# RG-LRU in a hybrid decoder block: the second gelu projection between the gates of the two blocks, with weights split up to two pieces ahead

## The chip, the cores and the metric

The kernel runs on one core of a Trainium2 chip. Its engines are TensorE (PE, with its weight loads listed as PEld), VectorE (DVE), ScalarE (ACT), GpSimd (POOL) and SyncE (SP), which here only issues loads. Each engine works through a queue of its own in a fixed order, and semaphores tie the queues together. Matrix products land in PSUM, which DVE and ACT can read. The metric is the time of one execution on the device, in microseconds, as the median of several runs.

## The reference

One decoder block on a sequence of 512 tokens, with 16 meta tokens ahead of them and a width of 1024. Two token mixers, HGRN2 and RG-LRU, read the same normalised input; their outputs are merged by sigmoid gates, and a mixture of 32 experts follows. The part that the change touches is the RG-LRU:

```python
    xc = conv(xb) + conv_b                       # causal, depthwise, width 4
    r = sigmoid(einsum('btni,nij->btnj', xh, w_r) + b_r)   # 8 blocks of 128
    i = sigmoid(einsum('btni,nij->btnj', xh, w_i) + b_i)
    log_a = -8 * r * softplus(-lam)
    a = exp(log_a)
    u = sqrt(-expm1(2 * log_a)) * (i * xc)
    h = scan(h_t = a_t * h_{t-1} + u_t)
    return h * gelu(yb)
```

Here `xb` and `yb` are 1024 columns each of the projection of the normalised input, called lx and ly below.

## The kernel before

Tokens lie along the free dimension and channels along the partitions. A projection of 128 channels takes eight steps of 128 input channels. For precision each operand of a large product is split into a high and a low part, and three products are added: high times high, high times low, low times high. The normalised input stays in buffers, split, for the whole mixer (`hnH`, `hnL`).

Weights come in pieces of 128 columns. The class `Weights` holds them in the order of use: `load` issues a load of two pieces (1 MB) on SP's queue into one of two `raw` buffers, and `prep` splits the next piece into one of three `hl` tiles, which are used in turn. In the RG-LRU the high half is a cast on ScalarE (L88) and the low half a subtraction on POOL (L91); in the merge behind it the cast is on DVE (L90). `dense` (L196) takes a ready piece, multiplies, and calls `prep` once when it is halfway through, so that the next piece is being split while the present one is in use. Gate weights of two blocks, for r and i, form one piece of half the width.

`lru` (L622) goes over the 8 blocks in pairs. For a pair it emits the projections lx of both blocks, whose output is convolved on DVE (L650) and split (L88, L91); then the tail of the pair before, called `finish` (L690): logarithms and exponentials on ScalarE, a product (L703), the scan over time (L704), a product with the gelu (L705) and a split on DVE, whose low half is on POOL; then the projections ly of both blocks, whose output becomes the gelu in four instructions, alternately on ScalarE and DVE (L673 to L676); then the gates of both blocks. `gates` (L656) fills four PSUM tiles with 12 short matmuls (L663); ScalarE reads them with a tanh (L665) into `RR` (r) and `iv` (i), and DVE multiplies (L667). `RR` and `TH` are one buffer each, which the tail of a pair reads and the gates of the next pair write.

All PSUM tiles come from one pool of eight. One lx output takes two, one ly output one, the gates of one block four. Between these steps the loop at L714 lets the last two heads of the HGRN2 take a step, one every five steps of the projections: a step multiplies scores for one level into a tile that is kept for two levels (L545, read on DVE in L561), in the first four levels a product of states into a tile of its own (L550, read in L553 or L555), and at the end the head's output (L566, L567, read in L576).

The framework plans the order on each engine when the kernel is built: the program's order is its priority, but an instruction that it believes to be held up lets later ones pass, and it gives PSUM tiles out in the order that it plans. So the convolution of lx (L650), which the program has ahead of the tail, stands between the tail's L703 and L704 in the trace.

After the RG-LRU comes the merge (L799): gate projections, projections of both mixers' outputs, and the output projection. As its buffers come free, the loads of the experts' weights start. Then come the routing and the experts.

Of the kernel before, what the change touches and what calls it, by code (L numbers as in the profile page):

```python
# [19 lines left out]
M = 16  # L20
N = T + M
D = 1024
KD = D // 128
# [7 lines left out]
PARTS = ((0, 256), (256, 528))  # L31
# [7 lines left out]
def hybrid_block_kernel(ctx: ExitStack, tc: tile.TileContext, x, meta, norm1_g, w_in, hg_lb,  # L39
# [21 lines left out]
    def add_slots(pool, names):  # L61
        for n in names:
            pool_of[n] = pool
            free.append(n)

    def uniq(name):
        seq[0] += 1
        return f"{name}_{seq[0]}"

    def slot(shape, dtype, name):  # L70
        s = free.pop(0)
        return pool_of[s].tile(shape, dtype, name=uniq(name), tag=s), s
# [4 lines left out]
    def ms(tag, shape, dtype, name):  # L77
        return misc.tile(shape, dtype, name=uniq(name), tag="m" + tag)

    def ps(shape, name, dtype=F32):  # L80
        return psum.tile(shape, dtype, name=name, tag="ps")
# [4 lines left out]
    def split(hi, lo, src, he, le):  # L86
        if he is ACT:
            ACT.activation(hi, src, AF.Copy)  # L88
        else:
            he.tensor_copy(hi, src)  # L90
        le.tensor_sub(lo, src, hi.bitcast(F32))  # L91
# [87 lines left out]
    W = Weights()  # L179
# [13 lines left out]
        W.columns(wub, 128 * j, DVE, POOL)  # L193
    W.rows(wout2, 128 * (KD - 2), DVE, POOL)

    def dense(outs, cols_, nk, aH, aL):  # L196

        wh, wl = W.next()
        for k in range(nk):
            if k == nk // 2:  # L200
                W.prep()
            for w, a in ((wh, aH), (wh, aL), (wl, aH)):
                for o, (c0, c1) in zip(outs, cols_):
                    PE.matmul(o[:, :c1 - c0], w[:, k, :], hsl(a, k, c0, c1),  # L204
                              start=(k == 0 and w is wh and a is aH),
                              stop=(k == nk - 1 and w is wl))
            yield

    def proj(all_tokens, use, parts=PARTS):
        if all_tokens:  # L210
            pp = [ps([128, b - a], "pj") for a, b in parts]
            yield from dense(pp, parts, KD, hnH, hnL)
            use(pp)
        else:
            p_ = ps([128, 512], "pj")
            yield from dense([p_], [(M, N)], KD, hnH, hnL)
            use(p_)

    def interleave(main, sides, every):
# [22 lines left out]
    hnH, hnL, hn_s = [], [], []  # L242
    for i in range(2):
        a, s = slot([128, 4, N], F32R, "hnH")
        b, s2 = slot([128, 4, N], F32R, "hnL")
# [4 lines left out]
    def hsl(lst, k, a, b):  # L250
        return lst[k // 4][:, k % 4, a:b]
# [85 lines left out]
    def col(nm, i=None):  # L337
        a, b = R[nm]
        return cols[:, a:b] if i is None else cols[:, a + i:a + i + 1]
# [264 lines left out]
    def add_ob():  # L604
        for lst, nm in ((obH, "obH"), (obL, "obL")):
            t_, s = slot([128, 4, T], F32R, nm)
            lst.append(t_)
            ob_s.append(s)
# [4 lines left out]
    def end_heads():  # L613

        for g_ in sides:
            run(g_)
        sides.clear()
        tp.__exit__(None, None, None)
        late = ctx.enter_context(tc.tile_pool(name="late", bufs=1, side="right", reuse_waits="tile"))
        add_slots(late, [f"t{i}" for i in range(NLATE)])  # L620

    def lru():  # L622
        L2 = ms("F", [128, 2, N], F32, "l2")
        iv = L2[:, 0]
        tail = None

        gp = tc.tile_pool(name="gelu", bufs=1, reuse_waits="tile")
        pool_of["g"] = gp.__enter__()
        for b0 in range(0, NB, 2):
            bs = (b0, b0 + 1)  # L630
            XC = ms("AH"[b0 // 2 % 2], [128, 2, N], F32, "xc")
            RR = ms("C", [128, 2, N], F32, "r")
            TH = ms("D", [128, 2, N], F32, "th")
            GE = (ms("E", [128, 2, T], F32, "ge") if b0 % 4 else
                  pool_of["g"].tile([128, 2, T], F32, name=uniq("ge"), tag="g"))
            XH = {}
            WG = []

            def use_lx(b):
                def f(pp):  # L640

                    xc = XC[:, b - b0]
                    for (a, c), p_ in zip(PARTS, pp):
                        ACT.activation(xc[:, a:c], p_[:, p_.shape[1] - (c - a):], AF.Identity,
                                       scale=col("cw", 24 + b), bias=col("cb", b))
                    for d in range(1, 4):
                        for (a, c), p_ in zip(PARTS, pp):
                            n = p_.shape[1]
                            o = xc[:, max(a, d):c]
                            DVE.scalar_tensor_tensor(o, p_[:, n - d - o.shape[1]:n - d], col("cw", 8 * (3 - d) + b), o,  # L650
                                                     op0=OP.mult, op1=OP.add)
                    xh = XH[b] = ms("BG"[b - b0], [128, 2, N], F32R, "xh")
                    split(xh[:, 0], xh[:, 1], xc, ACT, DVE)
                return f

            def gates(b):  # L656
                xh, i = XH[b], b - b0
                r, th = RR[:, i], TH[:, i]
                for gi, dst in enumerate((r, iv)):
                    pg = [ps([128, 272], "pg") for _ in PARTS]  # L660
                    for w, a in ((0, 0), (0, 1), (1, 0)):
                        for (c0, c1), p_ in zip(PARTS, pg):
                            PE.matmul(p_[:, :c1 - c0], WG[w][:, 2 * gi + i], xh[:, a, c0:c1], start=(w == 0 and a == 0), stop=(w == 1))  # L663
                    for (c0, c1), p_ in zip(PARTS, pg):
                        ACT.activation(dst[:, c0:c1], p_[:, :c1 - c0], AF.Tanh, scale=0.5, bias=hb[:, 8 * gi + b:8 * gi + b + 1])  # L665
                ACT.activation(th, r, AF.Tanh, scale=C4[:, b:b + 1], bias=C4[:, b:b + 1])
                DVE.scalar_tensor_tensor(XC[:, i], iv, 1.0, XC[:, i], op0=OP.add, op1=OP.mult)  # L667

            def use_ly(b):
                def f(p_):  # L670

                    c, ge = math.sqrt(2 / math.pi), GE[:, b - b0]
                    ACT.activation(ge, p_, AF.Square, scale=math.sqrt(0.044715 * c))  # L673
                    DVE.scalar_tensor_tensor(ge, ge, c, p_, op0=OP.add, op1=OP.mult)
                    ACT.activation(ge, ge, AF.Tanh)
                    DVE.scalar_tensor_tensor(ge, ge, 1.0, p_, op0=OP.add, op1=OP.mult)  # L676
                return f

            for b in bs:
                yield from proj(True, use_lx(b), PARTS4)  # L680
            if tail:
                tail()
            for b in bs:
                yield from proj(False, use_ly(b))
            WG += W.next()
            W.prep()
            for b in bs:
                gates(b)
                yield
            def finish(b0=b0, bs=bs, XC=XC, RR=RR, TH=TH, GE=GE):  # L690
                for i in range(2):
                    ACT.activation(L2[:, i], TH[:, i], AF.Ln, bias=1.0)
                    ACT.activation(TH[:, i], TH[:, i], AF.Ln, scale=2.0, bias=tiny)
                    DVE.tensor_sub(TH[:, i], TH[:, i], L2[:, i])
                if b0 == 4:
                    end_heads()
                    add_ob()
                for i, b in enumerate(bs):

                    av, u, ge = RR[:, i], TH[:, i], GE[:, i]  # L700
                    ACT.activation(av, av, AF.Exp, scale=NC4[:, b:b + 1], bias=NC4[:, b:b + 1])
                    ACT.activation(u, u, AF.Exp, scale=0.5, bias=nln2)
                    DVE.tensor_mul(u, u, XC[:, i])  # L703
                    DVE.tensor_tensor_scan(u, av, u, 0.0, op0=OP.mult, op1=OP.add)  # L704
                    DVE.scalar_tensor_tensor(ge, ge, 0.5, u[:, M:], op0=OP.mult, op1=OP.mult)  # L705
                    split(obH[b // 4][:, b % 4], obL[b // 4][:, b % 4], ge, DVE, POOL)

            tail = finish
        tail()
        gp.__exit__(None, None, None)  # L710
        late2 = ctx.enter_context(tc.tile_pool(name="late2", bufs=1, reuse_waits="tile"))
        add_slots(late2, ["u0"])
# [16 lines left out]
    def tk(lst, t, a=0, b=D):  # L729
        return lst[t // 2][:, t % 2, a:b]  # L730
# [389 lines left out]
    for p in range(last_p + 1):  # L1120
# [15 lines left out]
        if p == last_p:  # L1136
            gfb = ms("A", [128, D], F32, "gfb")
            for half in range(2):
                p_ = ps([128, 4, 128], "pgf")
# [27 lines left out]
    outs = [slot([128, D], F32, "o") for t in range(4)]  # L1167
# [12 lines left out]
    for t in range(4):  # L1180
        p_, hs = ps([128, 512], "pcb"), tk(h32, t, 512)
# [89 lines left out]
```

## Time and profile before

| | |
|---|---|
| median of 3 runs | 1009.46 us (1008.91 to 1009.81) |
| profiled execution, its own time | 1012.21 us |
| its span, from the first to the last instruction | 1010.4 us |
| mean granted TensorE clock | 0.968 |
| PE busy | 941.5 us (93%) |
| DVE busy | 449.7 us (45%) |
| ACT busy | 256.0 us (25%) |
| POOL busy | 246.1 us (24%) |
| read from memory | 250.89 MB |

Busy shares are averages over stages that differ: the mixer up to about 300 us, the merge to 486 us, and the experts. All times in rows below are microseconds from the start of the span. A granted clock of 1.00 is 2.4 GHz and 0.50 is 1.2 GHz; a value between is a mix of the two in a stretch.

### The profile page before, as it was taken

How to read it: one execution, taken by the hardware profiler on the slowest of the kernel's cores; microseconds unless marked ns; L12 is line 12 of the kernel's file. 1: busy time of each engine (PE TensorE's matmuls, PEld its weight loads, DVE VectorE, ACT ScalarE, POOL GpSimd, SP SyncE). 2: the span in 40 equal slices, each digit the busy share in tenths (PEclk: the TensorE clock that was granted, in tenths of full speed). 3: DMA queues.
4: the chain of work that ended last, by engine and by line, in shares of the span. 5: the costliest groups of instructions: out<-in, count | busy, mean ns of one | idle time of the engine just before them, and what ended most of it. 6: DMA issues, size and time to landing. Idle time of an engine off the chain costs nothing.

```text
span 1010.4 us, 12299 instructions
## 1 busy us (share of the span) xinstructions
PE 941.5 (93%) x4812; PEld 608.2 (60%) x4812; DVE 449.7 (45%) x931; ACT 256.0 (25%) x456; POOL 246.1 (24%) x167
## 2 busy tenths in 40 slices
PE   7989999979898999999949999999999999989885
PEld 6979998868876888888833444434334343433331
DVE  5667548767583333333442333333343343323323
ACT  6445536855860000000401010101101010110014
POOL 4543441334446454545300000000000000000002
PEclk9999999979898999999959999999999999999998
DMA  6221112212176231316978999999999999999992
GB/s 213 85 84 43 43 53 84 71 35 84 53 262 222 63 125 63 125 63 247 384 296 293 409 408 408 408 408 408 409 409 409 408 408 408 409 408 408 408 355 88
DMA packets 94297, 251.76 MB, mean 249 GB/s; under 512 B 6581, under 2 KB 39433, under 8 KB 94234
## 3 DMA queue, kind: packets, MB, share of 16 engines
q1 hardware_dynamic: 91352, 244.61, 63.5%
q0 software_dynamic: 2304, 4.20, 1.1%
q10 hardware_dynamic: 578, 2.10, 0.5%
q8 instruction: 40, 0.66, 0.3%
q14 instruction: 23, 0.19, 0.1%
HBM read 250.89 MB, written 4.19 MB: 252 GB/s over the span
## 4 chain that ended last, share of the span: by engine, by line
PE 76%; DVE 8%; DMA 7%; ACT 4%; POOL 2%; issue 2%; SPq 0%; POOLq 0%; DVEq 0%; ACTq 0%
PE pj L204 26%; PE put L1009 11%; PE pgt L1009 9%; PE py L1028 9%; PE pcb L1042 6%; DMA wx<-in_w_up_dram 6%; PE po L794 3%; PE pl L545 2%; PE pw L971 2%; PE pxs L1001 1%; PE po L1066 1%; PE pj L311 1%; POOL hl L91 1%; DVE th L703 1%; PE pht L1022 1%
## 5 line engine op out<-in xcount | busy, mean ns | idle before, releaser
L204 PE MATMUL pj<-hnH,hl 128*128 128x512 f32 (+1 forms) x960 | 253.7, 355 | 5.1 <-POOL hl L91 5.1
L91 POOL TENSOR_TENSOR hl<-raw,hl 128x1024 fp32r<-128x1024 f32 (+1 forms) x76 | 175.9, 2318 | 208.1 <-ACT hl L88 107.0
L204 PEld LDWEIGHTS pj<-hnH,hl 128*128 128x128 f32 x960 | 165.8, 195 | 29.3 <-POOL hl L91 6.9
L204 PE MATMUL pj<-hnL,hl 128*128 128x512 f32 (+1 forms) x480 | 150.0, 351 | 0.0
L1045 DVE TENSOR_TENSOR h<-h,pcb 128x512 f32<-128x512 f32 x124 | 77.5, 681 | 112.6 <-PE pcb L1042 112.6
L1009 PE MATMUL put<-wx,XS 128*64 128x512 f32 x512 | 121.1, 600 | 3.4 <-DMA wx<-in_w_up_dram 3.4
L1009 PE MATMUL pgt<-wx,XS 128*64 128x512 f32 x512 | 119.6, 606 | 1.9 <-DMA wx<-in_w_gate_dram 1.9
L978 POOL DMA_INDIRECT XG<-HD,idx x16 | 16.5, 1029 | 411.7 <-DVE sw L987 252.6
L1028 PE MATMUL py<-wx,HG 128*64 128x512 f32 x512 | 113.8, 596 | 0.7 <-ACT HG L1023 0.7
L204 PEld LDWEIGHTS pj<-hnL,hl 128*128 128x128 f32 x480 | 86.1, 194 | 10.2
L1009 PEld LDWEIGHTS pgt<-wx,XS 128*64 128x64 f32 x512 | 36.0, 139 | 71.1 <-issue 63.2
L1028 PEld LDWEIGHTS py<-wx,HG 128*64 128x64 f32 x512 | 35.2, 137 | 66.2 <-issue 61.1
L1009 PEld LDWEIGHTS put<-wx,XS 128*64 128x64 f32 x512 | 33.6, 136 | 67.3 <-issue 62.8
L1042 PE MATMUL pcb<-Y,OHT 128*128 128x512 f32 x248 | 68.1, 411 | 0.0
L1042 PEld LDWEIGHTS pcb<-Y,OHT 128*128 128x128 f32 x248 | 43.5, 188 | 39.3 <-issue 30.8
L1036 DVE SCALAR_TENSOR_TENSOR Y<-py,sw,Y 128x512 fp32r<-128x512 f32 x31 | 23.3, 751 | 91.7 <-ACT Y L1035 90.6
L90 DVE CAST hl<-raw 128x1024 fp32r<-128x1024 f32 (+1 forms) x40 | 31.7, 793 | 66.4 <-PE pj L204 64.6
L1023 ACT ACTIVATE HG<-pht 128x512 f32<-128x512 f32 x16 | 9.6, 598 | 182.5 <-PE pht L1022 182.4
L1035 ACT ACTIVATE Y<-py,sw 128x512 fp32r<-128x512 f32 x31 | 21.3, 688 | 102.5 <-PE py L1028 98.6
L204 PE MATMUL pj<-obH,hl 128*128 128x512 f32 x128 | 40.7, 394 | 0.0
L1014 ACT ACTIVATE HG<-pgt,sw 128x512 f32<-128x512 f32 x16 | 11.0, 687 | 107.4 <-PE pgt L1009 107.4
L88 ACT ACTIVATE hl<-raw 128x1024 fp32r<-128x1024 f32 (+1 forms) x36 | 36.1, 1006 | 7.1 <-PE pj L311 3.2
(259 smaller groups left out, 1116.5 us busy)
## 6 DMA issues: line engine op xcount, KB each, us to landing
wx<-in_w_up_dram SPq DMA_DIRECT2D x64, 1024.0 KB, 18.4
wx<-in_w_gate_dram SPq DMA_DIRECT2D x62, 1024.0 KB, 18.3
wx<-in_w_down_dram SPq DMA_DIRECT2D x60, 1024.0 KB, 19.0
raw<-in_w_in_dram SPq DMA_DIRECT2D x24, 1024.0 KB, 5.2
raw<-in_w_up_b_dram SPq DMA_DIRECT2D x4, 1024.0 KB
raw<-in_w_out_dram SPq DMA_DIRECT2D x4, 1024.0 KB
wx<-in_w_down_dram SPq DMA_DIRECT2D x8, 512.0 KB, 17.1
h<-in_x_dram SPq DMA_DIRECT2D x2, 1024.0 KB
```

Source lines behind the costliest of these rows:

```text
L88: ACT.activation(hi, src, AF.Copy)
L90: he.tensor_copy(hi, src)
L91: le.tensor_sub(lo, src, hi.bitcast(F32))
L204: PE.matmul(o[:, :c1 - c0], w[:, k, :], hsl(a, k, c0, c1), start=(k == 0 and w is wh and a is aH), stop=(k == nk - 1 and w is wl))
L545: PE.matmul(pl[:, li % 2, c], zc, halves(zc, m)[1], start=True, stop=True)
L794: PE.matmul(p_, mg[:, a, k, 128 * t:128 * t + 128], w[:, k, :], start=(k == 0 and a == 0 and w is wh), stop=(k == 1 and a == 1))
L1009: PE.matmul(p_[CAP * e:CAP * e + CAP], XS[:, k, CAP * e:CAP * e + CAP], weight(w2, e, k, 0), start=(k == 0), stop=(k == 7))
L1028: PE.matmul(p_[CAP * e:CAP * e + CAP], HT[:, 128 * k + CAP * e:128 * k + CAP * e + CAP], weight(w2, e, k, 512 * half), start=(k == 0), sto ...
L1035: ACT.activation(yh, p_, AF.Copy, scale=sw[:, 0:1])
L1036: DVE.scalar_tensor_tensor(Y[half][:, 1], p_, sw[:, 0:1], yh.bitcast(F32), op0=OP.mult, op1=OP.subtract)
L1042: PE.matmul(p_, oht[:, 128 * t:128 * t + 128], Y[half][:, i], start=(i == 0), stop=(i == 1))
L1045: DVE.tensor_add(hs, hs, p_)
```

## The change

For each pair, the ly projection of the first block is followed by that block's gates, then by the ly projection of the second block and that block's gates. The piece of weights for the second ly is taken from the list ahead of the gates' piece and handed to `proj` by hand. Ahead of the first ly two pieces are split, and `dense` splits a further piece halfway through only while fewer than two are ready, so that pieces are up to two ahead there and in all that follows.

```diff
-    def dense(outs, cols_, nk, aH, aL):
-
-        wh, wl = W.next()
+    def dense(outs, cols_, nk, aH, aL, w_=None):
+
+        wh, wl = w_ or W.next()
         for k in range(nk):
-            if k == nk // 2:
+            if k == nk // 2 and len(W.ready) < 2:
                 W.prep()
...
-    def proj(all_tokens, use, parts=PARTS):
+    def proj(all_tokens, use, parts=PARTS, w=None):
...
-            yield from dense([p_], [(M, N)], KD, hnH, hnL)
+            yield from dense([p_], [(M, N)], KD, hnH, hnL, w)
             use(p_)
...
             if tail:
                 tail()
-            for b in bs:
-                yield from proj(False, use_ly(b))
+
+            while len(W.ready) < 2:
+                W.prep()
+            yield from proj(False, use_ly(b0))
+            w_ly = W.next()
             WG += W.next()
+            gates(b0)
+            yield
+            yield from proj(False, use_ly(b0 + 1), w=w_ly)
+            gates(b0 + 1)
             W.prep()
-            for b in bs:
-                gates(b)
-                yield
+            yield
```

## Rows read from the trace of the kernel before

**Rows 1.** The page, DMA rate in 40 equal slices of the span.

```profile
GB/s 213 85 84 43 43 53 84 71 35 84 53 262 222 63 125 63 125 63 247 384 296 293 409 408 408 408 408 408 409 409 409 408 408 408 409 408 408 408 355 88
```

**Rows 2.** Windows: three pairs, start of merge, rest; busy by engine, clock, DMA.

```profile
173.30:218.70 45.40, 37.66 (x238) 34.53 (x238) 35.16 (x62) 31.35 (x47) 16.71 (x8) 0.88 0.19 59
218.70:257.20 38.50, 34.26 (x223) 31.50 (x222) 22.52 (x34) 23.66 (x50) 15.94 (x9) 0.94 0.17 56
257.20:289.10 31.90, 29.71 (x178) 27.21 (x178) 22.71 (x34) 20.85 (x36) 14.09 (x8) 0.92 0.45 156
289.10:317.20 28.10, 24.47 (x89) 19.09 (x88) 16.66 (x22) 13.77 (x20) 18.14 (x9) 0.82 0.61 210
317.20:486.00 168.80, 168.80 (x730) 136.88 (x730) 53.12 (x82) 12.85 (x21) 83.40 (x40) 1.00 0.38 133
```

**Rows 3.** Waits of PE, 155 to 350 us: total, times, longest.

```profile
PE pg L663 <- DVE sc L561: 5.1, 1, 5.1
PE pj L204 <- POOL hl L91: 4.2, 3, 3.3
PE pg L663 <- DVE ge L676: 4.1, 3, 1.5
PE pg L663 <- DVE on L576: 2.0, 1, 2.0
PE pg L663 <- ACT r L665: 1.7, 2, 1.0
```

**Rows 4.** Timeline of PE, 160 to 235 us: start, duration, instructions, idle before.

```profile
196.44 0.50 PE L204 MATMUL pj<-hnH,hl 128*128 128x512 f32 x1 [0.52 <-POOL hl L91]
196.78 1.00 PE L545 MATMUL pl<-z 128*128 128x64 f32 x8
...
203.42 0.89 PE L663 MATMUL pg<-xh,hl 128*128 128x256 f32 x6
...
210.54 1.45 PE L663 MATMUL pg<-xh,hl 128*128 128x272 f32 x5 [5.09 <-DVE sc L561]
```

**Rows 5.** Timeline of DVE, 158 to 222 us.

```profile
197.49 2.47 DVE L650 SCALAR_TENSOR_TENSOR xc<-pj,cols,xc 128x255 f32<-128x255 f32 x6
199.89 2.38 DVE L704 TENSOR_TENSOR_SCAN th<-r,th 128x528 f32<-128x528 f32 x2
...
204.68 0.33 DVE L555 SCALAR_TENSOR_TENSOR st<-st,gend,pS 128x128 f32<-128x128 f32 x1
...
209.97 0.42 DVE L561 COPY_PREDICATED sc<-lmask,pl 128x256 f32<-128x256 uint8 x1
```

**Rows 6.** Timeline of ACT, 158 to 222 us.

```profile
211.01 0.63 ACT L675 ACTIVATE ge<-ge 128x512 f32<-128x512 f32 x1 [0.49 <-DVE ge L674]
...
214.48 0.84 ACT L665 ACTIVATE r<-pg,hb 128x256 f32<-128x256 f32 x2
```

**Rows 7.** The chain that ended last, a piece of the merge.

```profile
358.48 38.82 PE pj L204 x168
```

**Rows 8.** Timeline of DVE, 222 to 330 us.

```profile
233.72 4.29 DVE L703 TENSOR_TENSOR th<-th,xc 128x528 f32<-128x528 f32 x2 [0.24 <-ACT th L702]
...
249.08 0.69 DVE L576 TENSOR_TENSOR on<-po,rs 128x512 f32<-128x512 f32 x1 [3.39 <-POOL rs L107]
...
251.06 0.69 DVE L676 SCALAR_TENSOR_TENSOR ge<-ge,pj 128x512 f32<-128x512 f32 x1 [0.70 <-ACT ge L675]
...
299.74 1.49 DVE L703 TENSOR_TENSOR th<-th,xc 128x528 f32<-128x528 f32 x2
```

**Rows 9.** Timeline of POOL, 222 to 330 us.

```profile
233.14 4.30 POOL L91 TENSOR_TENSOR hl<-raw,hl 128x1024 fp32r<-128x1024 f32 x2 [9.41 <-ACT hl L88]
...
308.82 7.44 POOL L91 TENSOR_TENSOR hl<-raw,hl 128x1024 fp32r<-128x1024 f32 x3
```

**Rows 10.** Timeline of ACT, 222 to 330 us.

```profile
284.96 0.63 ACT L675 ACTIVATE ge<-ge 128x512 f32<-128x512 f32 x1 [6.31 <-DVE ge L674]
...
291.65 0.83 ACT L666 ACTIVATE th<-r,spt 128x528 f32<-128x528 f32 x1
```

## The prediction, made before the changed kernel ran

> **What bounds the kernel now.** I read the page's 40 slices first [rows 1]. From slice 23 on (about 556 us) DMA moves 408 or 409 GB/s in every slice until near the end: the expert stage lives on its weight stream, which can only start in earnest when the merge gives its buffers free. So a microsecond taken out ahead of the merge's end should move the whole expert stage forward by a microsecond. In the slices ahead of it (1 to 18) DMA moves far less, so time can be won there.
>
> Then the stretches of the RG-LRU stage [rows 2]: the second, third and fourth pair of blocks (from the first lx matmul to the last gate matmul), the first 28 us of the merge, and the rest of the merge. The rest of the merge is solid (168.80 us busy of 168.80, clock 1.00): a rigid block that only shifts. The pairs are not. PE idles 45.40 - 37.66 = 7.7 us in the second, 38.50 - 34.26 = 4.2 in the third, 31.90 - 29.71 = 2.2 in the fourth, and 28.10 - 24.47 = 3.6 at the start of the merge. The clock costs more on top: (1 - 0.88) x 45.40 = 5.4 us, then 2.3, 2.6 and 5.1, as an upper estimate since part of it falls on idle time. DMA is busy 0.17 to 0.45 of the pairs, so loads don't set their length.
>
> Third, the waits of PE in the stage [rows 3]. All but the POOL ones stand ahead of the gates' matmuls (L663), and what ends them is an instruction of DVE or ScalarE that reads an older PSUM tile: the gates don't wait for data but for one of the 8 PSUM tiles. The timeline of the second pair shows it [rows 4]: six gate matmuls (two tiles) run at 203.42, then one more, then PE stands for 5.09 us until DVE's L561 of 209.97 [rows 5]; later waits name ly's L676 [rows 3]. Counting tiles at 204: two ly outputs (held until L676), one state product (until L555, 204.68), one score tile (until L561, 209.97), one younger score tile for each of the two heads, and the two gate tiles just filled: eight. DVE can't free any, for it is in the tail of the previous pair (L703 to L705, among them the scans of L704 [rows 5]) and the heads' products queued behind it; and ScalarE can't free the gate tiles, because its in-order queue holds L675 of ly first, which starts at 211.01, and reaches the gates' L665 at 214.48 [rows 6].
>
> **The change part by part.** No instruction is added or removed: the same matmuls, splits and loads run in another order.
>
> *Gates of block b0 ahead of the second ly.* A ly output costs one tile for 24 matmuls, 24 x 38.82 / 168 = 5.5 us by the merge's like ones [rows 7]; a block's gates cost four tiles for 12 matmuls of 0.89 / 6 = 0.15 us, 1.8 us [rows 4]. Today PE spends its long jobs first and then asks for eight tiles in a row while DVE is shut. After, it asks for four, then for one with 5.5 us of cover, then for four; and gate tiles are read by ScalarE alone, so they come back without DVE.
>
> Second pair by the old clock. The wait of 0.52 us ahead of 196.44 [rows 4] falls on ly1's third matmul, the first with the low half of its weights, so ly0 ends near 195.5. Five tiles are taken then: two of lx1 (until L650 ends, 197.49 + 2.47 = 199.96), ly0, one state product, one score tile. Two gate tiles run to 196.4, a head's step [rows 4] takes the eighth tile and PE to 197.4; then PE waits for L650: 2.6 us. The other two gate tiles run to 200.9. The second ly needs a tile: ScalarE frees it with the tanh into r, a buffer that the tail's first scan still reads until 199.89 + 2.38 / 2 = 201.1; plus 0.84 / 2 for the tanh that is 201.5, a wait of 0.6. ly1 and a head's step end at 208.0; gates(b1) runs seven matmuls to 209.1 and then needs L561's end, 210.4: 1.3. Idle left 2.6 + 0.6 + 1.3 = 4.5, saved 7.7 - 4.5 = 3.2. The clock: 4.2 us of idle cost the third pair 2.3, so I take that, saved 5.4 - 2.3 = 3.1. Sum 6.3. Bounds: if ScalarE's queue has L675 ahead of the gates' tanh, ly1's tile comes only with L555's end at 205.0, idle is 2.6 + 4.1, and 1 us is saved; if every wait and the clock's loss vanish, 7.7 + 5.4 = 13.1.
>
> Third pair. PE waits there for ly0's L676, for L576 on a head's output, and for L665 [rows 3]. ly0, ly1 and two head outputs hold four tiles; DVE stands before L576 and has L674 and L676 of ly0 behind it, to 251.06 + 0.69 [rows 8]. After the change the second four tiles no longer need the last head output, since those of gates(b0) are back by then: its 2.0 us are saved. The other waits I leave, and the clock's 2.3 too, since the fourth pair's 2.2 us of idle cost 2.6. Bounds 0 and 4.2 + 2.3 = 6.5.
>
> Fourth pair. Here what PE gains is lost again at once: the merge's first weights need POOL, which is behind the tail's splits. What counts is the last tail, which holds POOL until it splits weights at 308.82 [rows 9]; the merge's long wait of 3.3 us [rows 3] ends with those. That tail begins when ScalarE is through with the gates, 291.65 + 0.83 = 292.5 [rows 10]. After, PE without its 2.2 us of idle would end the gates at 289.1 - 2.2 = 286.9, and ScalarE, where L675 of ly0 still starts at 284.96, four tanh and L666 later: 286.9 + 1.7 + 0.8 = 289.4, so 3.1 earlier at best. I take 2.5; bounds 0 and 2.2 + 2.6 = 4.8. The merge's own wait follows the tail and stays: 0.
>
> First pair: no tail precedes it and none of the waits of [rows 3] is known there: 0.
>
> *Weights up to two pieces ahead.* The ring of three split tiles stays, so a split still can't start before the matmuls three pieces back have ended; the condition only gives a split (a cast on ScalarE, a subtraction on POOL, at times a load on SP's queue) an earlier place. This is needed, for the gate weights are now due one ly earlier. The wait of 0.52 us for POOL in the second ly is in the idle time already. In the merge the lead changes nothing: PE has no idle time there [rows 2]. SP's loads move up with the splits; 0. What hides these is POOL's spare time, 45.40 - 16.71 us in the second pair; without it each split of 128x1024 would cost its 7.44 / 3 = 2.5 us [rows 9].
>
> Sum: 6.3 + 2.0 + 2.5 = 10.8 us. The profiled execution took 1012.21 us (span 1010.4), the runs' median is 1009.46, 0.27% less; the sum is made against the span and I take the same microseconds off the median: 998.7, with a span of about 999.6.
>
> **The rivals.**
>
> *The stall only moves (chance 0.20).* The order on each engine is planned, not the program's alone, and the plan may undo the move: ScalarE's order keeps L675, which waits for DVE, ahead of the tanh of gates(b0), and PE stands before ly1 instead of inside the gates. For it: that order today [rows 6]. Against: the gates' matmuls now come a ly earlier, so a planner that queues by readiness should place their tanh earlier. It gives the lower bounds, 1 + 0 + 0: 1008.5.
>
> *Earlier splits hold DVE up (chance 0.14): slower.* POOL's two splits at 233.14 to 237.44 stretched two multiplications of the tail to 4.29 us, against 1.49 without POOL beside them [rows 8, 9]. The change brings the next pair's first split, 2.5 us, from behind the tail into it: its tile is free as soon as ly0's matmuls end. If DVE's tail grows by 2.5 in three pairs and nothing is saved, it is 1009.5 + 7.5 = 1017.0. It decides from the point where what a pair saves is under 2.5. Against: the second split of the burst, the gates', is half as wide, and the one in the way now moves out ahead. The Trainium skill, SBUF — State Buffer, "SBUF: two separate sides", says that a DVE instruction with two SBUF inputs and a GpSimd instruction lock each other out for a whole instruction; by that rule the trace agrees, 4.29 against 1.49.
>
> *Nearly all comes back (chance 0.08).* If ScalarE always frees gate tiles in time, idle and clock go: 13.1 + 6.5 + 4.8 = 24.4, and 985. Against: lx's tiles hold PE until L650 whatever ScalarE does.
>
> **How the numbers follow.** The forecast has 0.58, and its own range is a gain of 5 to 20 us, 989.5 to 1004.5. A change within 0.2% (2 us) can't be told from none. Faster: 0.58 + 0.08 + 0.08 of the first rival (it may still save 2 to 5) = 0.74; the same 0.12; slower 0.14. The range, 988 to 1011, leaves out the slower rival and some of the largest gain, under 2 in 10.
>
> **What would show it.** Right: the 5.09 us wait ahead of L663 gone, gate matmuls of b0 between the two ly, PE's idle in the second pair near 4.5 us, the clock in the pairs at 0.92 or more, the merge's solid part some 11 us earlier and as long as before. Wrong: PE waiting ahead of the second ly (L204) for L555 or L665; more table loads on ScalarE; tail multiplications on DVE over 4 us in two pairs; a merge that starts earlier and waits longer for POOL.

## The result, and the profile after

| | before | after |
|---|---|---|
| median of the runs taken together | 1009.63 us (4 runs) | 998.5 us (997.48 to 999.0, 4 runs) |
| ratio | | 0.9884, 95% interval 0.9864 to 0.9903 |
| profiled execution, its own time | 1012.21 us | 998.75 us |
| its span | 1010.4 us | 997.0 us |
| long wait ahead of the merge ends at | 311.65 us | 298.43 us |
| from there to the end of the span | 698.75 us | 698.57 us |

The kernel is 1.2% faster, 11.1 us by the medians; a second set of runs gave 996.94 us and a ratio of 0.9874 [0.9858, 0.989]. The two profiled executions differ by 13.4 us of span, more than the medians do, since the one of before took 2.6 us more than its median. Nearly all of the 13.4 (13.2) is there before the merge's solid part begins. The lines of the changed kernel's tail are numbered 5 higher (L703, L704 and L705 are now L708, L709 and L710).

The page, clock and DMA rate in 40 slices, of the kernel after:

```profile
PEclk9999999999988999999959999999999999999998
...
GB/s 215 77 92 45 44 53 85 62 45 85 218 236 100 96 91 99 92 99 312 389 258 328 409 407 408 408 409 408 409 409 409 408 408 408 408 408 409 409 356 87
```

The weight stream of the experts runs at 407 to 409 GB/s from slice 23 on, as in [rows 1]; that slice began at 22 x 1010.4 / 40 = 556 us and begins now at 22 x 997.0 / 40 = 548.

Windows of the kernel after, cut at the same events as [rows 2]: three pairs, start of the merge, the rest. Columns: length, busy time of PE, PEld, DVE, ACT and POOL, clock, DMA share, GB/s.

```profile
173.60:213.20 39.60, 35.27 (x230) 31.57 (x229) 33.07 (x60) 28.67 (x42) 14.59 (x7) 0.96 0.19 61
213.20:246.20 33.00, 33.00 (x233) 30.89 (x233) 20.30 (x34) 25.09 (x54) 15.83 (x9) 1.00 0.23 73
246.20:273.30 27.10, 27.05 (x178) 24.74 (x177) 21.02 (x33) 19.71 (x34) 13.88 (x9) 1.00 0.51 187
273.30:304.00 30.70, 24.49 (x88) 19.07 (x87) 19.48 (x25) 14.32 (x21) 19.87 (x10) 0.84 0.63 225
304.00:472.80 168.80, 168.80 (x729) 136.83 (x729) 54.79 (x82) 12.84 (x21) 83.28 (x40) 1.00 0.37 126
```

Against [rows 2] the pairs are 5.8, 5.5 and 4.8 us shorter. PE's idle fell from 7.7 to 4.3 us in the second, from 4.2 to 0 in the third, from 2.2 to 0 in the fourth; the granted clock is 0.96, 1.00 and 1.00 where it was 0.88, 0.94 and 0.92. The start of the merge got worse: 30.70 us for 28.10, and 6.2 us of idle for 3.6. The rest of the merge is 168.80 us in both. DVE shows something that no one asked of it: 33.07 + 20.30 + 21.02 = 74.4 us of busy time in the three pairs for work that took 35.16 + 22.52 + 22.71 = 80.4 before. A part of that has only moved: the start of the merge has 19.48 us for 16.66, so that over the four stretches, with 152 instructions in either kernel, it is 93.9 us for 97.1.

Waits of PE of the kernel after, 155 to 350 us: total, times, longest.

```profile
PE pj L204 <- POOL hl L91: 6.2, 2, 3.3
PE pj L204 <- DVE st L555: 2.3, 1, 2.3
PE pl L545 <- DVE sc L561: 1.2, 1, 1.2
PE pg L663 <- POOL hl L91: 0.6, 1, 0.6
PE pg L663 <- DVE xc L650: 0.2, 1, 0.2
```

Of [rows 3] the 5.1 us for L561, the 4.1 for L676, the 2.0 for L576 and the 1.7 for ScalarE's L665 are gone from the gates. What is left in the pairs is 2.3 + 1.2 + 0.6 + 0.2 = 4.3 us, all in the second. The two waits for POOL are the merge's.

Timeline of PE of the kernel after, from the second pair's gates to the merge:

```profile
195.97 0.75 PE L663 MATMUL pg<-xh,hl 128*128 128x256 f32 x4
197.32 0.63 PE L663 MATMUL pg<-xh,hl 128*128 128x256 f32 x3 [0.60 <-POOL hl L91]
198.11 0.88 PE L663 MATMUL pg<-xh,hl 128*128 128x272 f32 x5 [0.17 <-DVE xc L650]
...
202.09 0.79 PE L204 MATMUL pj<-hnH,hl 128*128 128x512 f32 x1 [2.27 <-DVE st L555]
...
208.50 1.08 PE L545 MATMUL pl<-z 128*128 128x64 f32 x8 [1.20 <-DVE sc L561]
...
211.57 1.63 PE L663 MATMUL pg<-xh,hl 128*128 128x256 f32 x12
...
235.79 1.65 PE L663 MATMUL pg<-xh,hl 128*128 128x256 f32 x12
...
276.76 1.01 PE L204 MATMUL pj<-hnH,hl 128*128 128x512 f32 x2 [2.95 <-POOL hl L91]
...
298.43 1.22 PE L204 MATMUL pj<-hnH,hl 128*128 128x512 f32 x2 [3.26 <-POOL hl L91]
```

The first block's gates (195.97 to 199) stand ahead of the second ly, which waits 2.27 us; the second block's gates run in one go at 211.57, as all later ones do. The merge waits twice for its weights.

Timeline of ACT of the kernel after, the tanh of the first block's gates:

```profile
201.90 0.47 ACT L665 ACTIVATE r<-pg,hb 128x256 f32<-128x256 f32 x1 [1.27 <-DVE th L709]
208.05 0.43 ACT L480 ACTIVATE e<-e 128x256 f32<-128x256 f32 x1 [5.68 <-DVE e L479]
208.38 0.47 ACT L665 ACTIVATE r<-pg,hb 128x272 f32<-128x272 f32 x1
```

ScalarE frees one gate tile at 201.90, and then its in-order queue stands before a head's L480 until 208.05: the other three gate tiles are held for 6 us more. The kernel lives with it, since DVE's L555 (201.72 to 202.05, where it was 204.68 in [rows 5]) gives a tile instead.

### The profile page after: what moved, and what is told of

Its sections match the earlier page's. It is cut to its first block, busy times and chain, and to the rows that moved or that the text cites. A ratio compares the mean times of both kernels' runs of the same rounds, so it can differ in the third digit from the quotient of the medians.

```text
span 997.0 us, 12289 instructions
## 1 busy us (share of the span) xinstructions
PE 936.4 (94%) x4812; PEld 602.8 (60%) x4812; DVE 448.3 (45%) x931; ACT 255.9 (26%) x456; POOL 246.0 (25%) x167
## 4 chain that ended last, share of the span: by engine, by line
PE 80%; DVE 7%; DMA 5%; ACT 4%; POOL 2%; issue 2%; SPq 0%; POOLq 0%; DVEq 0%; ACTq 0%
PE pj L204 27%; PE put L1014 11%; PE pgt L1014 10%; PE py L1033 10%; PE pcb L1047 7%; DMA wx<-in_w_up_dram 4%; PE po L799 3%; PE pl L545 2%; PE pw L976 2%; PE pxs L1006 1%; PE po L1071 1%; PE pj L311 1%; PE pht L1027 1%; POOL hl L91 1%; DMA XG<-HD,idx 1%
## 5 line engine op out<-in xcount | busy, mean ns | idle before, releaser
L91 POOL TENSOR_TENSOR hl<-raw,hl 128x1024 fp32r<-128x1024 f32 (+1 forms) x76 | 174.9, 2303 | 202.2 <-ACT hl L88 100.0
L204 PEld LDWEIGHTS pj<-hnH,hl 128*128 128x128 f32 x960 | 163.9, 192 | 33.5 <-POOL hl L91 8.5
```

The costliest lines, as they stand in the source:

```text
L204: PE.matmul(o[:, :c1 - c0], w[:, k, :], hsl(a, k, c0, c1), start=(k == 0 and w is wh and a is aH), stop=(k == nk - 1 and w is wl))
```

## The experiments

**Order alone, and lead alone.** The change has two parts. The first kernel has the new order with weights one piece ahead, as before:

```diff
-            if k == nk // 2 and len(W.ready) < 2:
+            if k == nk // 2:
...
-            while len(W.ready) < 2:
-                W.prep()
...
             gates(b0 + 1)
-            W.prep()
```

> The order alone: the second ly between the gates, but weights split one piece ahead as before. Theory (PSUM tiles come free in a better order): nearly the whole gain stays, 998 to 1002 us, up to 3 us given back where the gate weights' low half is now late. Rival (the gain is that of earlier splits, which leave DVE's tail alone): 1007 to 1010.

Measured: 1005.28 us, ratio 0.996 [0.9948, 0.9972] (8 runs): a third of the gain, and in the range of neither the theory nor the rival. Waits of PE of this kernel, 155 to 350 us, and its timeline in the fourth pair:

```profile
PE pj L204 <- POOL hl L91: 6.4, 2, 3.3
PE pg L663 <- ACT hl L88: 2.9, 2, 1.6
PE pg L663 <- POOL hl L91: 2.8, 2, 2.0
PE pj L204 <- DVE st L555: 0.9, 1, 0.9
```

```profile
267.52 0.75 PE L663 MATMUL pg<-xh,hl 128*128 128x256 f32 x4 [1.55 <-ACT hl L88]
270.25 2.13 PE L663 MATMUL pg<-xh,hl 128*128 128x256 f32 x8 [1.98 <-POOL hl L91]
```

Now the gates wait for their own weights, 2.9 us for ScalarE's high half and 2.8 for POOL's low half.

The second kernel is the old one, order untouched, with the lead:

```diff
-            if k == nk // 2:
+            if k == nk // 2 and len(W.ready) < 2:
...
+            while len(W.ready) < 2:
+                W.prep()
```

> The lead alone: both ly ahead of both gates as before, but two pieces split ahead. Theory (PSUM tiles): within 2 us of the kernel before, 1007.5 to 1011.5, with the waits ahead of the gates still there. Rival (earlier splits): 998 to 1002.

Measured: 1002.15 us, ratio 0.9929 [0.9907, 0.9951]. My theory, that the lead by itself is worth nothing, is wrong; it is worth more than the order. The product of the two ratios, 0.996 x 0.9929 = 0.9889, is about the whole change's 0.9884, but the stages show that the parts don't simply add up:

| last matmul of | before | order alone | lead alone | both |
|---|---|---|---|---|
| second pair | 218.70 | 214.6 | 215.5 | 213.20 |
| third pair | 257.20 | 247.7 | 249.5 | 246.20 |
| fourth pair | 289.10 | 280.05 | 278.1 | 273.30 |
| end of the merge's long wait | 311.65 | 305.30 | 302.18 | 298.43 |

The order alone shortens the third pair as far as both together do (33.1 and 33.0 us), but leaves the fourth at 32.3, where the waits of 1.55 and 1.98 us stand. With the lead alone the second pair ends 3.2 us earlier and is 4.1 shorter (its first lx matmul is at 174.23 us, where it was at 173.33); the third and fourth are 4.5 and 3.3 shorter. Under the new order the lead is worth most in the fourth pair (32.3 to 27.1), under the old one in the third (38.5 to 34.0).

**What the lead gives in the old order.** With the lead the second ly's split on POOL runs at 185.50 us in the second pair; before it ran at 193.99 for 2.40 us, beside the tail's two multiplications, which took 2.68 us from 194.88. The tail of the third pair in the kernel with the lead alone (timeline of DVE; L705 there is L703 of before):

```profile
229.19 1.34 DVE L705 TENSOR_TENSOR th<-th,xc 128x528 f32<-128x528 f32 x2 [0.64 <-ACT th L704]
```

That is 1.34 us for the two that took 4.29 in [rows 8]. To see what POOL's split by itself costs, this kernel takes the old order and the old lead, and fills the low half of the second ly's weights with zeros on POOL. It leaves that correction out of the projection; every matmul still runs.

```diff
-        le.tensor_sub(lo, src, hi.bitcast(F32))
+        if le == "zero":
+            POOL.memset(lo.bitcast(F32), 0.0)
+        else:
+            le.tensor_sub(lo, src, hi.bitcast(F32))
...
-        W.columns(w_in2, 3072 + 128 * b, ACT, POOL)
+        W.columns(w_in2, 3072 + 128 * b, ACT, (POOL, "zero"))
```

> The order and the lead of before, but the low half of the second ly's weights in each pair is filled with zeros by POOL instead of being subtracted, so POOL reads no SBUF there (that correction is left out of the result). Theory (the lead helps in the old order because that split no longer stands on the tail's multiplications on DVE): L703 takes about 1.5 us for two in the second and third pair, and 2 to 6 us of the 7 that the lead alone gave are seen, 1002 to 1006. Rival (the lead helps by ScalarE's order, with fewer table loads, or by the plan): L703 falls but the time stays within 1.5 us of before.

Measured: 1002.96 us, ratio 0.9939 [0.9918, 0.9961]. Timeline of DVE of this kernel (L706 is L703 of before), and its first waits of PE:

```profile
196.14 1.34 DVE L706 TENSOR_TENSOR th<-th,xc 128x528 f32<-128x528 f32 x2 [1.14 <-ACT th L705]
...
233.51 1.33 DVE L706 TENSOR_TENSOR th<-th,xc 128x528 f32<-128x528 f32 x2 [0.24 <-ACT th L705]
```

```profile
PE pg L666 <- DVE sc L564: 5.1, 1, 5.1
```

Without the subtraction DVE's multiplications are back at 1.3 us, and the kernel is 6 us faster, nearly as much as by the lead. The second pair starts 1.3 us later here, at 174.58, and the three pairs are 1.1, 3.6 and 2.4 us shorter than before, where the lead alone gave 4.1, 4.5 and 3.3. In the second pair the wait for the score tile, L564 here, is still 5.1 us. This kernel also spares POOL 1.45 us for each such piece (0.95 for the filling, 2.40 for the subtraction), so not all of its gain need be DVE's.

What the lead gives beyond that in the second pair goes with ScalarE. Its table loads (ACT_TABLE_LOAD, 1.28 us each) are six in that pair before and in the kernel with zeros, and four with the lead alone. There the convolution starts at 192.93 us, where [rows 5] have 197.49, and L555 comes at 200.82 in place of 204.68. Timeline of DVE of the kernel with the lead alone:

```profile
192.93 2.56 DVE L650 SCALAR_TENSOR_TENSOR xc<-pj,cols,xc 128x255 f32<-128x255 f32 x6
...
200.82 0.34 DVE L555 SCALAR_TENSOR_TENSOR st<-st,gend,pS 128x128 f32<-128x128 f32 x1
```

That the loads are the cause is not shown: no run changes them alone.

**Is it tiles?** The prediction says that the gates wait for one of 8 PSUM tiles. One tile is withheld through the stage, first in the old kernel, then in the changed one; a matmul and a one-element multiplication are added.

```diff
+        hold = ps([128, 512], "hold")
+        PE.matmul(hold[:, :128], ident, ident, start=True, stop=True)
...
+                if b0 == 6:
+                    DVE.tensor_tensor(warm, hold[:, :1], GE[:, 1, :1], op=OP.mult)
```

> The kernel before with one of the eight PSUM tiles withheld for the whole of the RG-LRU (one small product goes into it at the start, its first column is read after the last tail). Theory (PSUM tiles): the waits ahead of the gates begin a tile earlier and grow, 2 to 10 us slower than before, 1012 to 1020. Rival (splits and DVE's port): tiles don't matter, within 1 us of before.

> The changed kernel with one of the eight PSUM tiles withheld in the same way. Theory (PSUM tiles): the second pair waits longer ahead of the second ly and waits may come back in the third, 3 to 10 us slower than the changed kernel, 1001 to 1009, and still under the kernel before with a tile withheld. Rival (splits and DVE's port): within 1 us of the changed kernel, 997.5 to 999.5.

The changed kernel got slower, to 1003.91 us, ratio 0.9961 [0.9947, 0.9975], 5.4 us above the 998.5 and, by the two ratios, 0.8%. Its waits of PE:

```profile
PE pl L545 <- DVE st L555: 4.3, 1, 4.3
PE pj L204 <- DVE sc L561: 3.8, 1, 3.8
```

Two waits of the kernel after, 2.3 us for L555 and 1.2 for L561, became waits of 4.3 and 3.8 us for the same two: what PE lacks in the second pair is a tile. The old kernel, though, got faster by 0.2%, 1006.01 us, ratio 0.9981 [0.9971, 0.9991], against my expectation. Its second pair did get longer (it ends at 222.15 us, with 4.6 us ahead of the gates for L561 and 3.4 for ge's L678, which is L676 of before), but its third and fourth pair take 33.5 and 28.4 us, where [rows 2] have 38.5 and 31.9. With a tile less the planner put the work of the engines in another order, and those two pairs came out shorter; which part of the new order does it is not traced. So a count of tiles gives the price of a wait, and not that of a plan.

**Fewer tiles for a block's gates.** A block's gates take four tiles of 256 and 272 columns. Three would do: 512 columns for each gate, and one shared by the two gates' 16 columns.

```diff
+                pm = ps([128, 2, M], "pg")
...
-                    pg = [ps([128, 272], "pg") for _ in PARTS]
+                    pg = ps([128, 512], "pg")
...
-                        for (c0, c1), p_ in zip(PARTS, pg):
+                        for c0, c1, p_ in ((M, N, pg), (0, M, pm[:, gi])):
```

In the changed kernel:

> The changed kernel with three PSUM tiles for a block's gates in place of four: 512 columns of r, 512 of i, and the 16 columns of the meta tokens of both in a shared tile; the same number of matmuls and tanh. Theory (PSUM tiles still hold PE in the second pair): the waits of 2.27 and 1.20 us there shrink, 1 to 4 us faster than the changed kernel, 994.5 to 997.5. Rival (what is left there is DVE's backlog, whatever the tiles): within 1 us.

In the old one:

> The kernel before with three PSUM tiles for a block's gates in place of four. Theory (the gates of before wait for tiles): six tiles in a row in place of eight, the waits ahead of the gates shrink by 2 to 6 us, 1002 to 1007. Rival (DVE's backlog sets the length of a pair, whatever the tiles): within 1.5 us of before.

Measured: 1006.77 us, ratio 0.9982 [0.9969, 0.9995], some 8 us above the changed kernel; and 1010.69 us, 1.0019 [1.0009, 1.003]. Both expected a gain, and neither kernel has one. Wait of PE in the first of the two:

```profile
PE pg L664 <- ACT r L666: 10.1, 3, 7.0
```

The shared tile ties the second gate's products to ScalarE's reading of the first, and the longest of these waits alone is 7.0 us. The next kernel issues all of a block's matmuls ahead of its first tanh, which takes that tie away:

```diff
+                pm, pgs = ps([128, 2, M], "pg"), []
+                for gi in range(2):
+                    pgs.append(ps([128, 512], "pg"))
...
+                for gi, dst in enumerate((r, iv)):
+                    for c0, c1, p_ in ((M, N, pgs[gi]), (0, M, pm[:, gi])):
+                        ACT.activation(dst[:, c0:c1], p_, AF.Tanh, scale=0.5, bias=hb[:, 8 * gi + b:8 * gi + b + 1])
```

> The changed kernel with three PSUM tiles for a block's gates, as before, but with all of a block's matmuls ahead of its first tanh, so that the shared tile no longer makes the products for i wait until ScalarE has read those for r. Theory (the earlier try was slowed by that coupling alone, and tiles still hold PE in the second pair): the waits of the gates for ScalarE go, 0 to 4 us faster than the changed kernel. Rival (short matmuls of 16 columns and longer tanh cost more than a tile is worth): 1 to 4 us slower than the changed kernel.

Measured: 1003.57 us, ratio 0.9939 [0.9923, 0.9956], still 6.6 us above the 996.94 of the changed kernel on that chip, and slower than even the rival had it. Timeline of PE and windows of this kernel:

```profile
210.81 3.98 PE L664 MATMUL pg<-xh,hl 128*128 128x512 f32 x12 [2.49 <-ACT e L480]
240.42 2.11 PE L664 MATMUL pg<-xh,hl 128*128 128x512 f32 x12
```

```profile
214.79:251.93 37.14, 37.14 (x233) 34.50 (x234) 21.05 (x37) 25.83 (x54) 16.22 (x10) 0.92 0.20 65
...
212.00:216.00 4.00, 4.00 (x16) 3.60 (x15) 3.14 (x8) 3.97 (x8) 0.72 (x1) 0.50 0.00 0
216.00:222.00 6.00, 6.00 (x33) 6.00 (x33) 1.72 (x3) 5.97 (x11) 4.17 (x2) 0.58 0.15 44
```

A block's 12 gate matmuls take 2.11 us where the even halves take 1.65 (235.79 above): about 0.5 more for a block, 1 for a pair. The third pair is 37.14 us with no idle time, 4.1 longer than after; its clock is 0.92 for 1.00, and (1 - 0.92) x 37.14 = 3.0 us with 1.0 for the gates makes up the difference. The loss is at the pair's start: the granted clock is 0.50 (1.2 GHz) from 212 to 216 us and 0.58 to 222, behind a wait of 2.49 us (PE was busy for 3.51 of the 6 us ahead of 212), while PE is busy all the time. In the second pair, which is 41.19 us long for 39.60, PE's idle time did fall, from 4.3 to 3.1 us. So tiles were saved, and matmul time and clock were paid.

**The merge's first weights.** What the pairs gain is partly given back ahead of the merge, where two waits for POOL of 2.95 and 3.26 us stand. Three kernels change the changed kernel there. The first has the last tail's low halves on DVE in place of POOL, whose queue has them ahead of the merge's splits:

```diff
-                    split(obH[b // 4][:, b % 4], obL[b // 4][:, b % 4], ge, DVE, POOL)
+                    split(obH[b // 4][:, b % 4], obL[b // 4][:, b % 4], ge, DVE, DVE if b0 == 6 else POOL)
```

> The changed kernel with the low half of the last tail's output (two subtractions of 128x512) on DVE in place of POOL. Theory (what the fourth pair saves is lost at the merge's start, where POOL splits weights only after that tail): the waits for POOL of 2.95 and 3.26 us shrink, 2 to 6 us faster than the changed kernel, 992.5 to 996.5. Rival (the merge's start waits for its own casts on DVE or its loads): within 1 us of it.

The second has the pieces of the merge's first two gate projections cast by ScalarE and not by DVE:

```diff
-        W.columns(w_in2, 4096 + 128 * j, DVE, POOL)
+        W.columns(w_in2, 4096 + 128 * j, DVE if j else ACT, POOL)
...
-        W.columns(w_in2, 5120 + 128 * j, DVE, POOL)
+        W.columns(w_in2, 5120 + 128 * j, DVE if j else ACT, POOL)
```

> The changed kernel with the high halves of the merge's first two gate projections (four pieces) cast on ScalarE in place of DVE. Theory (at the merge's start the casts queue on DVE behind the tail, and POOL's splits behind the casts and the tail's own): both waits for POOL, 2.95 and 3.26 us, go or halve, with the clock's loss behind them, 4 to 9 us faster than the changed kernel, 989 to 994. Rival (POOL's queue, which has the tail's low halves first, sets both waits whoever casts): within 1 us of the changed kernel.

Both edits in one kernel:

> The same, and the low half of the last tail's output on DVE. Theory: as the kernel with the casts on ScalarE or up to 2 us faster, since POOL is then free at the second wait. Rival (the two subtractions lengthen DVE's tail, which the first projection of the second mixer waits for): 0 to 2 us slower than it.

And the changed kernel once more, beside the last two:

> The changed kernel once more, as the measure for the other three on this chip: 997 to 1000 us, 0.986 to 0.991 of the kernel before.

Measured: 995.31 us, ratio 0.988 [0.9851, 0.9908]; 995.52 us, 0.986 [0.9843, 0.9877]; both 989.98 us, 0.9807 [0.9793, 0.9822]; the changed kernel 996.94 us, 0.9874 [0.9858, 0.989]. The first two can't be told from the changed kernel, their intervals overlap with its own; together they are 7 us faster than it and beat both kernels of this study. That is 5.5 us below the casts alone, where the theory had up to 2. Timelines of PE: the first with the tail on DVE, the second with ScalarE's casts, the third with both.

```profile
277.31 0.73 PE L204 MATMUL pj<-hnH,hl 128*128 128x512 f32 x2 [2.93 <-POOL hl L91]
...
297.03 0.73 PE L204 MATMUL pj<-hnH,hl 128*128 128x512 f32 x2 [1.28 <-POOL hl L91]
```

```profile
297.33 1.22 PE L204 MATMUL pj<-hnH,hl 128*128 128x512 f32 x2 [5.73 <-POOL hl L91]
```

```profile
293.91 0.73 PE L204 MATMUL pj<-hnH,hl 128*128 128x512 f32 x2 [1.57 <-POOL hl L91]
```

Each edit takes one of the two waits. ScalarE's casts alone take the first (2.95 to nothing) and the second grows to 5.73, since the same POOL queue is behind it; DVE's low halves alone take 2 us of the second. With both, one wait of 1.57 us is left and the merge starts 4.5 us earlier than after; the other 2.3 us of the span's 6.8 lie behind that point, and I have not traced them.

## Why the prediction was right, and where not

The forecast was 998.7 us, the runs say 998.5. Its sum was 10.8 us against a span that fell by 13.4, so that agreement is closer than the working deserves. It is luck in another way too: the sum stands for the order and has the lead at nothing, while by themselves the order gave 3.1 us (1008.35 to 1005.28) and the lead 6.2. Term by term:

- **Second pair, 6.3: right in size, 5.8 measured.** Idle left is 4.3 us (4.5 forecast), the clock 0.96, the 5.09 us wait is gone. The single waits are others: 0.6 us for the gates' weights from POOL and 0.2 for L650 in place of 2.6 for L650, which ends 1.5 us earlier than in [rows 5] (196.00 + 2.46 = 198.46); 2.27 ahead of the second ly in place of 0.6; 1.2 for L561 in place of 1.3, on a head's products in place of the gates. The mark of PE waiting ahead of the second ly for L555 did appear. The first rival's mechanism is there: ScalarE's queue holds the other gate tiles behind L480 until 208.05. It cost 2.27 us and not 4.1 since L555 came 3 us earlier than in [rows 5]. Of the 5.8 us the order alone gives 4.4. One thing the reading of the 5.09 us wait left out: DVE was not only late but stretched. Timeline of DVE of the kernel before, between the L555 and the L561 of [rows 5]:

```profile
204.94 1.23 DVE L490 TENSOR_TENSOR z<-kk,e 128x256 f32<-128x256 f32 x1
206.09 1.48 DVE L493 TENSOR_TENSOR z<-qT,e 128x256 f32<-128x256 f32 x1
207.49 2.56 DVE L479 TENSOR_TENSOR e<-g 128x256 f32<-128x256 f32 x1
```

  These three take 5.27 us while POOL splits from 204.50 to 209.77, and 0.42 us each at 185.65, 185.98 and 191.48, where POOL is idle. So, as an estimate from these rows, 4.0 of the 5.09 us are the stretching that the prediction priced for the tail's multiplications alone. After, L490 and L479 still take 2.59 and 1.50 us, and PE waits 1.2 for the L561 behind them.
- **Third pair, 2.0: the mis-sized term, 5.5 measured.** I took out the wait for the last head output and left the rest and the clock's loss. No wait is left and the clock is 1.00. The bound of 6.5, every wait and the clock's loss, was the near one. Both parts of the change reach most of it alone: 5.4 us by the order, 4.5 by the lead.
- **Fourth pair, 2.5: right as a net, 2.2 measured.** The pair is 4.8 us shorter (my upper bound), and 2.6 come back ahead of the merge, where the text said that what PE gains is lost again. The mark "a merge that starts earlier and waits longer for POOL" did appear: 6.2 us in two waits, where it was 0.30 and 3.34. The kernels with the merge's first weights on other engines show that POOL's queue and DVE's casts hold it.
- **Weights two ahead, 0: the step that failed.** Alone it is worth 0.7% in the old order, 6 us by the medians of that comparison. The text says that the lead "only gives a split [...] an earlier place" and that POOL's spare time hides it. The place was what mattered: beside the tail the split cost DVE 4.29 us for 1.3, in the third pair, and DVE is what the gates' tiles wait for. In the second pair the kernel with zeros has only 1.1 of the lead's 4.1 us. Under the new order the lead also pays by the weights of the gates, which the order alone waits 5.7 us for.
- **Earlier splits hold DVE up (0.14): its sign was reversed.** The mechanism is real and its row was read rightly. But the lead takes splits out of DVE's way: from the second pair through the start of the merge, over 152 instructions in each kernel, DVE is busy for 97.1 us before, 100.3 with the order alone, 91.8 with the lead alone and 93.9 after. After, the third pair's two multiplications take 0.94 and 0.71 us. With the order alone they are short too, 1.44 for both, but there the two scans behind them take 3.44 us for 2.40, beside the gates' split. The text had weighed this, "the one in the way now moves out ahead", and gave it no price.
- **A microsecond ahead of the merge is one at the end: right.** From the end of the merge's long wait to the end of the span it is 698.75 us before, 698.57 after, 699.2 with the order alone and 698.8 with the lead alone. In the kernels that change the merge's first splits it is less, 693.9 to 697.3.
- **Nearly all comes back (0.08):** it did in the third and fourth pair, not in the second, nor ahead of the merge.
- **First pair, 0:** it ends 0.3 us later. **More table loads:** six in the second pair's stretch, as before.

What is open: how much of the lead's gain is DVE's multiplications and how much is POOL being free for the next piece, since the kernel with zeros spares POOL as well; whether the two table loads make the rest of its second pair; and why the planner finds a better order with one tile less.

## What to carry to other kernels

When a change moves the time at which a side engine does its work, price that work where it stands today, not only where it goes: a subtraction of 2.4 us on POOL that seems free may stretch another engine's critical stretch by 3. Where a planner orders the engines, price a tile or a lead by a run, for a withheld tile made one order slower and the other, by 0.2%, faster. And look at what the gain runs into next: two edits that did nothing measurable alone gave 7 us together, since each eased one of two waits in a row on the same queue.

## What was not expected of the hardware

POOL beside DVE also stretches instructions with one input. After, two casts of weights on DVE start while a POOL subtraction runs, and end 0.3 to 0.6 us behind it. Timeline of DVE of the kernel after:

```profile
274.43 2.83 DVE L90 CAST hl<-raw 128x1024 fp32r<-128x1024 f32 x1
...
277.77 2.22 DVE L90 CAST hl<-raw 128x512 fp32r<-128x512 f32 x1
...
283.89 0.42 DVE L90 CAST hl<-raw 128x512 fp32r<-128x512 f32 x1
...
306.59 0.69 DVE L90 CAST hl<-raw 128x1024 fp32r<-128x1024 f32 x1 [10.41 <-PE pj L204]
```

And of POOL, the subtractions beside the first two:

```profile
273.90 2.80 POOL L91 TENSOR_TENSOR hl<-raw,hl 128x1024 fp32r<-128x1024 f32 x1
277.33 2.38 POOL L91 TENSOR_TENSOR hl<-raw,hl 128x1024 fp32r<-128x1024 f32 x1 [0.63 <-DVE hl L90]
```

Such casts take 0.69 us (1024 elements) and 0.42 (512) with POOL idle, at 306.59 and 283.89, and 2.83 and 2.22 beside it. It isn't always DVE that is longer: a cast of 1024 at 292.09 takes 0.69 us too, while POOL's two subtractions of 128x512 that began at 291.92 take 3.71, where two at 234.98 take 2.66. The multiplications of the tail show the same with two inputs, 4.29 against 1.3 for a pair. The Trainium skill, SBUF — State Buffer, "SBUF: two separate sides", names both cases in which DVE and GpSimd lock each other out, a DVE instruction in a mode that uses two ports and one with two SBUF inputs beside a GpSimd instruction that reads SBUF. By that rule the traces agree for the multiplications; no row says in which mode a cast ran, but 1024 elements in 0.69 us are twice the rate of a DVE subtraction of 528 (L91, 0.70). The prediction had used only the second case.

A matmul of 16 columns costs nearly as much as one of 264. In the kernel with three tiles a block's twelve take 2.11 us, 0.35 for 512 and 16 columns; 512 alone take 0.23 (38.82 / 168, [rows 7]), which leaves 0.12 for the 16. Of the even halves each takes 1.65 / 12 = 0.14. Either has a weight load of its own, 0.19 us.
